# Reordering VectorE in a chunked WKV kernel: a state chain ahead of a rounding that waits for its load, and one rounding moved by a slot

## Chip, cores and metric

The kernel runs on one core of one Trainium2 chip. The metric is the device time of a run in microseconds. The time before is 293.12 us, the median of 3 runs (293.1 to 293.28). The profiled execution has a span of 292.3 us; times of day inside the trace are counted from the start of that span.

## The reference

For each of 16 sequences and each of 256 channels a recurrence runs over 2048 time steps. It keeps a numerator `aa`, a denominator `bb` and a running maximum `pp`:

```python
ww = u + kk;  qq = max(pp, ww)
e1 = exp(pp - qq);  e2 = exp(ww - qq)
output = (e1 * aa + e2 * vv) / (e1 * bb + e2 + 1e-08)
ww = pp - w + kk;  qq = max(ww, kk)
e1 = exp(ww - qq);  e2 = exp(kk - qq)
aa = e1 * aa + e2 * vv;  bb = e1 * bb + e2;  pp = qq
```

So every output is a weighted mean of the values v seen so far, with weights that decay by w a step and a bonus u for the present step. The inputs k and v and the output are 33.5 MB each.

## The kernel before

**Tiling.** The time axis is cut into 16 chunks of 128 steps, and a chunk into 4 pieces of 4 sequences each. A piece n (0 to 63) is a tile of 128 partitions (the steps) by 4 x 256 elements (sequence, channel), 512 KB for k and as much for v. Pieces n with the same n // 4 make up one chunk; four slots in a row are called a turn below.

**One piece.** Within a chunk the recurrence is done with matrices over the step axis. `round_k` (L176, VectorE) rounds k to the matmul's 32-bit type into `km`; `logs` (L185 and L191, TensorE) makes two tables of logarithms in PSUM banks 0 to 3; `exps` (L204, ScalarE) turns them into weights in the ring `EZR`, which holds 12 pieces; `cast_v` (L209, VectorE) rounds v to bf16 into `vb`; `times_v` (L214, VectorE) multiplies weights and v. `sums` (L238, TensorE) adds up the piece for the chunk's state.

**The outputs** follow LAG = 10 slots later. `den` (L341, TensorE) sums the denominators into banks 4 and 5; `recip` (L347 and L349, ScalarE) takes logarithm and exponential of the negative, that is the inverse, into `rd`; `num` (L354, TensorE) sums one half of the numerators into bank 6, and `mult` (L358, VectorE) multiplies that half by the inverse. Both halves use the one bank, so `num` of the second half waits for `mult` of the first, and so on. `store` (L361) writes `rd` out.

**The state.** Once per chunk a chain of small operations carries the state of the recurrence over: `copy_sums`, `turn`, `state_logs`, `state_frames`, `state_scan`, `state_offsets`, `state_weights` (L290, ScalarE, makes `G`), then `state_chain` (four VectorE operations, L299 to L304, the last of which writes `CB`), `turn_back` (L320, TensorE, transposes `CB`), `inject` (L326 on VectorE, then four small transfers, L331, into the ring's rows) and `state_next`. The next chunk's outputs need the injected rows.

**What sets the order.** The order of instructions is written out by hand: `K` keeps the program's order on each engine, and each engine takes its queue strictly in order. The table `plan` says, for each chunk, at which slot and at which named place of the slot each state function stands; `small_work(n, place)` runs what is due there. Slots 0 to 9 are a warm-up without outputs; slots 10 to 63 are the main loop; then come 11 short slots that only produce outputs. In the main loop VectorE's order in a slot is: `mult` of the first half (of piece n-11), the place "mid", `round_k(n+2)`, one, two or no `cast_v`, `mult` of the second half, the place "scan", `times_v(n)`, the place "chain". Before the change the casts stand as follows: slots with n%4 = 0 and 1 round v of piece n+1, n%4 = 2 rounds none, n%4 = 3 rounds v of n and of n+1.

**Loads and buffers.** The SP queue issues in slot n the load of v of piece n+5, the load of k of piece n+6 and the store of piece n-13, in that order. v has 5 load buffers, so the load of v(n+5) waits until `cast_v(n)` has read v(n); k has 6, and its buffer is freed by `round_k`, which runs two slots ahead of the piece. `vb` has 4 buffers and `rd` has 8.

For chunk 1 the chain is due at slot 10, the first of the main loop, at place "chain": behind `round_k(12)` and `times_v(10)`.

Of the kernel before, what the change touches and what calls it, by code (L numbers as in the profile page):

```python
# [15 lines left out]
def kernel(  # L16
# [17 lines left out]
    NP = 4 * NST  # L34
    RING = 12
    AHEAD = 6
    LAG = 10
# [29 lines left out]
    def load(n):  # L67
        if n - 1 < NP:
            load_v(n - 1)
        if n < NP:  # L70
            load_k(n)
# [3 lines left out]
    def matrix(name, dt):  # L75
        return consts.tile([128, 128], dt, tag=name, name=name)

    def fill(ap, value):
        K(DVE.memset(ap.bitcast(F32) if ap.dtype == F32R else ap, value))
# [68 lines left out]
    def out_matrices(*names):  # L148
        if "L" in names:
            for h in range(2):  # L150
                fill(Lx[HS * h:HS * h + HS, HS * (1 - h):HS * (2 - h)], 0.0)
        for name in names:
            x, f = I1 if name[0] == "I" else Lx, RS if name[-1] == "N" else 1.0
            mats[name] = matrix(name, BF16)
            K(DVE.tensor_single_scalar(mats[name], x, f, op=ALU.mult))
# [8 lines left out]
    DENB, NUMB, MISC = PS[:, 4:6, :], PS[:, 6, :], PS[:, 7, :]  # L164
# [6 lines left out]
    def ez(n):  # L171
        return EZR[:, :, n % RING]

    def round_k(n):
        km = consts.tile([128, 4, Dm], F32R, tag=f"km{n % 2}", name="km") if n < 2 else KM[n - 2]
        K(DVE.tensor_copy(km, kr_of.pop(n)))  # L176
        KM[n] = km

    def logs(n):
        km = KM[n].rearrange("p (i n) d -> p i (n d)", i=2)  # L180

        def rows(q):
            for i in range(2):
                g = 32 * (2 * q + i)
                K(PE.matmul(half(n, q)[:, i, :], CO[g:g + 32, :],  # L185
                            WU[g:g + 32, :].unsqueeze(1).broadcast_to([32, 2, Dm]), start=True, stop=False,
                            tile_position=(g, 0), skip_group_check=True))

        def steps(q):
            for i in range(2):  # L190
                K(PE.matmul(half(n, q)[:, i, :], (NLE, NLZ)[q], km[:, i, :], start=False, stop=True,  # L191
                            skip_group_check=True))

        rows(0)
        rows(1)
        steps(0)
        steps(1)

    def exps(n):
        if n < TURNS:  # L200
            for q in range(2):
                K(SC.activation(ez(n)[:, q], half(n, q), ACT.Exp))  # L202
        else:
            K(SC.activation(ez(n)[:, 0:2], PS[:, 0:4, :].rearrange("p (q i) x -> p q i x", q=2), ACT.Exp))  # L204

    def cast_v(n):
        vb = vbpool.tile([128, 4, Dm], BF16, tag="vb", name="vb")
        vr = vr_of.pop(n)
        K(DVE.tensor_copy(vb, vr))  # L209
        VB[n] = vb  # L210

    def times_v(n):
        vb = VB.pop(n).rearrange("p (i n) d -> p i (n d)", i=2)
        K(DVE.tensor_mul(ez(n)[:, 2:4], ez(n)[:, 0:2], vb.unsqueeze(1).broadcast_to([128, 2, 2, D])))  # L214
# [16 lines left out]
    def sums(n):  # L231
        c, p = divmod(n, 4)
        t = MISC[:, 0:Dm]
        for o in range(2):
            x = 24 - 16 * o - 2 * p
            for j in range(4):
                q, i = divmod(j, 2)
                K(PE.matmul(t[32 * j:32 * j + 32, :], mats["OH"][:, x:x + 32],  # L238
                            ez(n)[:, 2 * q, i, Dm * o:Dm * o + Dm],
                            start=p == 0 and o == 0, stop=p == 3 and o == 1,  # L240
                            tile_position=(0, 32 * j), skip_group_check=True))
# [102 lines left out]
    def recip(n, between=lambda: None):  # L344
        rd = rpool.tile([128, 2, D], F32, tag="rd", name="rd")
        for i in (slice(0, 1), slice(1, 2)) if n == NP - 1 else (slice(0, 2),):
            K(SC.activation(rd[:, i, :], DENB[:, i, :], ACT.Ln, scale=RS))  # L347
            between()
            K(SC.activation(rd[:, i, :], rd[:, i, :], ACT.Exp, scale=-1.0))  # L349
        RD[n] = rd  # L350

    def num(n, bank, i):
        for m, q in (("LN", 2), ("IdN", 3)):
            K(PE.matmul(bank, mats[m], ez(n)[:, q, i, :], start=q == 2, stop=q == 3, skip_group_check=True))  # L354

    def mult(n, bank, i):
        rd = RD[n]
        K(DVE.tensor_mul(rd[:, i, :], bank, rd[:, i, :]))  # L358

    def store(n):  # L360
        K(SP.dma_start(out=rows_of(out, n), in_=RD.pop(n).rearrange("p i (n d) -> p (i n) d", n=2)))  # L361
# [10 lines left out]
    for c in range(NST):  # L372
        s = 4 * c + 3
        plan = [(s + 1, "act" if s + 1 < LAG else "recip", copy_sums), (s + 1, "pe", turn),
                (s + 2, "act", state_logs), (s + 2, "mid", state_frames), (s + 2, "scan", state_scan), (s + 2, "scan", state_offsets),
                (s + 3, "recip", state_weights), (s + 3, "chain", state_chain),
                (s + 4, "nums", turn_back), (s + 4, "mid", inject), (s + 4, "mid", state_next)]
        if c == 0:
            plan = [(s + 1, "act", copy_sums), (s + 1, "pe", turn), (s + 1, "pe", state_logs),
                    (s + 1, "round", state_frames), (s + 1, "round", state_scan), (s + 1, "round", state_offsets),  # L380
                    (s + 2, "act", state_weights), (s + 2, "round", state_chain),
                    (s + 3, "pe", turn_back), (s + 3, "round", inject), (s + 3, "round", state_next)]
        if c == 1:
            plan = [(s + 1, "act", copy_sums), (s + 1, "pe", turn), (s + 2, "act", state_logs),
                    (s + 2, "round", state_frames), (s + 2, "round", state_scan), (s + 2, "round", state_offsets)] + plan[6:]
        if c == NST - 1:
            plan = [(s + 1, "copy", copy_sums), (s + 1, "turn", turn),
                    (s + 1, "post", state_logs), (s + 1, "mid", state_frames), (s + 1, "mid", state_scan), (s + 1, "mid", state_offsets),
                    (s + 2, "post", state_weights), (s + 2, "first", state_chain),
                    (s + 3, "turn", turn_back), (s + 3, "first", inject)]  # L390
        for slot, where, f in plan:
            later.setdefault((slot, where), []).append((f, c))

    def small_work(n, where):
        for f, c in later.pop((n, where), []):
            f(c)

    def idle_matmuls(n, bank):
        for _ in range(n):
            K(PE.matmul(bank, idle[:, 0:128], idle, start=True, stop=True, skip_group_check=True))  # L400
# [9 lines left out]
    for n in range(LAG):  # L410

        load(n + AHEAD)
        exps(n)
        if n % 4 == 0 and n:
            sums(n - 1)
        small_work(n, "act")
        small_work(n, "logs")
        logs(n + 1)
        if n % 4:
            sums(n - 1)  # L420
        small_work(n, "pe")
        idle_matmuls(2, NUMB)
        times_v(n)
        small_work(n, "chain")
        round_k(n + 2)
        small_work(n, "round")
        cast_v(n + 1)
        if n < 4:
            (state_start, lambda: out_matrices("L"), lambda: out_matrices("IdN", "LN"),
             lambda: out_matrices("Id"))[n]()  # L430
    for n in range(LAG, NP):

        q, qp = n - LAG, n - LAG - 1
        load(n + AHEAD)

        if qp >= 2:
            store(qp - 2)
        if qp >= 0:
            num(qp, NUMB, 0)
        den(q)  # L440
        small_work(n, "nums")
        exps(n)
        small_work(n, "act")
        if qp >= 0:
            mult(qp, NUMB, 0)
        small_work(n, "mid")
        if n + 2 < NP:
            round_k(n + 2)

        if n % 4 == 3:  # L450
            cast_v(n)
        if n + 1 < NP:
            if n % 4 != 2:
                cast_v(n + 1)
        else:
            times_v(n)
        if qp >= 0:
            num(qp, NUMB, 1)

        sums(n - 1)  # L460
        recip(q, lambda: small_work(n, "recip"))
        if qp >= 0:
            mult(qp, NUMB, 1)
        small_work(n, "scan")
        if n + 1 < NP:
            times_v(n)
            small_work(n, "chain")
            logs(n + 1)
        else:
            den(q + 1)  # L470
        small_work(n, "pe")
# [5 lines left out]
    for n in range(NP, NP + LAG + 1):  # L477

        q, qp = n - LAG, n - LAG - 1
# [52 lines left out]
```

## Time and profile before

| what | value |
|---|---|
| time, median of 3 | 293.12 us |
| span of the profiled execution | 292.3 us |
| busy: TensorE / VectorE / ScalarE / GpSimd | 257.5 / 261.9 / 258.4 / 113.9 us |
| moved by DMA, mean rate over the span | 101.53 MB, 347 GB/s |
| `cast_v` (L209) | 64 x 693 ns |
| `round_k` (L176) | 64 x 688 ns; its engine idle 2.3 us before it, for the load |
| `mult` (L358) | 118 instructions, mean 735 ns; its engine idle 13.8 us before it |
| `times_v` (L214) | 64 x 1227 ns |
| `exps` in the main loop (L204) | 54 x 1873 ns; idle 7.6 us before it |
| load of k or v, from issue to landing (median) | 8.3 and 8.2 us |

The profile is read like this. A timeline line gives the start in us, the duration, the engine, the line of the kernel, the operation, output and inputs, and in brackets how long the engine had been idle and what released it. "PE" is TensorE, "DVE" VectorE, "ACT" ScalarE, "POOL" GpSimd, "SPq" the queue that issues loads and stores. Durations on one engine overlap a little at their ends: a 128x1024 rounding has a record of 0.69 us, but the next instruction starts 0.60 us after it. In the windows view a line gives a stretch of the span, its length, the busy time and count of each engine (PE, PEld, DVE, ACT, POOL), then the granted TensorE clock, the share of the 16 DMA engines' time that packets took, and GB/s.

### The profile page before, as it was taken

Reading aid. Unit: us, or ns where it says so; the run is one execution under the profiler, and the core shown is the slowest. Engines: PE = TensorE matmul, PEld = TensorE weight load, DVE = VectorE, ACT = ScalarE, POOL = GpSimd, SP = SyncE. Lnnn points to the kernel's source line nnn. Section 1 sums busy time; section 2 is a strip of 40 time slices with the busy share of each in tenths; the row PEclk is TensorE's granted clock in tenths of the full one; section 3 lists DMA queues with packets and bytes.
Section 4 is the critical chain, followed back from the end, with each engine's and each line's share of the span. In section 5 each row is a group of like instructions: output and inputs, shape, how many; then the busy total and the mean of one; then the engine's idle time right before and its main releaser. Section 6 shows DMA issues by size and latency. Waiting matters only on the chain. (4 is left out here: it accounts for less than half of the span.)

```text
span 292.3 us, 4981 instructions
## 1 busy us (share of the span) xinstructions
PE 257.5 (88%) x1662; PEld 119.7 (41%) x1694; DVE 261.9 (90%) x453; ACT 258.4 (88%) x253; POOL 113.9 (39%) x212
## 2 busy tenths in 40 slices
PE   6976896998989899998989899998989899998881
PEld 2332442534444354444444354444444354433330
DVE  4698989899999999999999999999999999986853
ACT  2765685999999999999999999999999999999892
POOL 7000434153555535253555535253555535242200
PEclk9999997999999999999999999999999999999998
DMA  5999999999999999999999999999999999974686
GB/s 191 356 348 349 348 332 349 334 365 364 378 375 374 380 375 382 379 378 380 380 377 382 380 380 380 377 371 378 379 378 380 370 375 381 370 247 151 222 284 215
DMA packets 103521, 101.53 MB, mean 347 GB/s; under 512 B 4156, under 2 KB 103496, under 8 KB 103496
## 3 DMA queue, kind: packets, MB, share of 16 engines
q1 hardware_dynamic: 101144, 100.42, 100.7%
q0 software_dynamic: 2048, 0.53, 0.8%
q8 instruction: 13, 0.21, 0.3%
q10 hardware_dynamic: 304, 0.27, 0.3%
q14 instruction: 12, 0.10, 0.1%
HBM read 67.12 MB, written 33.55 MB: 344 GB/s over the span
## 5 line engine op out<-in xcount | busy, mean ns | idle before, releaser
L204 ACT ACTIVATE EZR<-PS 128x2048 bf16<-128x2048 f32 x54 | 101.1, 1873 | 7.6 <-PE PS L191 4.9
L358 DVE TENSOR_TENSOR rd<-PS,rd 128x512 f32<-128x512 f32 (+1 forms) x118 | 86.5, 735 | 13.8 <-PE PS L354 7.9
L214 DVE TENSOR_TENSOR EZR<-EZR,vb 128x2048 bf16<-128x2048 bf16 x64 | 78.5, 1227 | 0.7
L349 ACT ACTIVATE rd<-rd 128x1024 f32<-128x1024 f32 (+1 forms) x65 | 67.8, 1043 | 1.2
L347 ACT ACTIVATE rd<-PS 128x1024 f32<-128x1024 f32 (+1 forms) x65 | 65.6, 1010 | 1.4 <-PE PS L341 1.3
L331 POOL DMA_DIRECT2D EZR<-cb x64 | 40.1, 632 | 61.1 <-DVE cb L326 42.3
L354 PE MATMUL PS<-EZR,LN 128*128 128x512 bf16 x128 | 48.7, 380 | 12.8 <-DVE rd L358 10.0
L191 PE MATMUL PS<-km,NLE 128*128 128x512 f32 x128 | 47.2, 450 | 4.1 <-DVE km L176 4.1
L176 DVE CAST km<-kr 128x1024 fp32r<-128x1024 f32 x64 | 44.0, 688 | 2.3 <-DMA kr<-in_k_dram 2.3
L209 DVE CAST vb<-vr 128x1024 bf16<-128x1024 f32 x64 | 43.3, 693 | 2.7 <-DMA vr<-in_v_dram 2.4
L354 PE MATMUL PS<-EZR,IdN 128*128 128x512 bf16 x114 | 43.1, 378 | 0.0
L191 PE MATMUL PS<-km,NLZ 128*128 128x512 f32 x128 | 40.5, 398 | 0.0
L341 PE MATMUL PS<-EZR,L 128*128 128x512 bf16 x127 | 37.8, 378 | 1.8 <-ACT rd L347 1.8
L341 PE MATMUL PS<-EZR,Id 128*128 128x512 bf16 x114 | 35.0, 379 | 0.1
L269 POOL TENSOR_TENSOR F<-LL,LL 128x32 f32<-128x32 f32 x13 | 9.5, 733 | 62.0 <-ACT LL L260 62.0
L185 PE MATMUL PS<-WU,CO 32*128 32x512 bf16 x256 | 27.3, 388 | 3.1 <-DVE WU L406 1.6
L238 PE MATMUL PS<-EZR,OH 128*32 128x256 bf16 x512 | 26.3, 280 | 2.4 <-issue 0.4
L191 PEld LDWEIGHTS PS<-km,NLE 128*128 128x128 f32 x128 | 19.2, 190 | 19.2 <-issue 12.7
L191 PEld LDWEIGHTS PS<-km,NLZ 128*128 128x128 f32 x128 | 24.3, 190 | 5.7
L202 ACT ACTIVATE EZR<-PS 128x1024 bf16<-128x1024 f32 x20 | 19.4, 1019 | 7.9 <-PE PS L191 7.9
L354 PEld LDWEIGHTS <-IdN 128*128 128x128 bf16 x128 | 12.4, 97 | 26.1 <-issue 23.7
L354 PEld LDWEIGHTS <-LN 128*128 128x128 bf16 x128 | 12.8, 100 | 18.5 <-issue 11.5
(71 smaller groups left out, 204.5 us busy)
## 6 DMA issues: line engine op xcount, KB each, us to landing
kr<-in_k_dram SPq DMA_DIRECT2D x64, 512.0 KB, 8.3
vr<-in_v_dram SPq DMA_DIRECT2D x64, 512.0 KB, 8.2
out_dram<-rd SPq DMA_DIRECT2D x63, 512.0 KB, 8.1
EZR<-cb POOLq DMA_DIRECT2D x64, 8.0 KB, 5.2
out_dram<-rd SPq DMA_DIRECT2D x2, 128.0 KB, 3.1
out_dram<-rd ACTq DMA_DIRECT2D x2, 128.0 KB, 3.3
wuf<-in_w_dram ACTq DMA_DIRECT2D x1, 8.0 KB
wuf<-in_u_dram SPq DMA_DIRECT2D x1, 4.0 KB
```

The costliest lines, as they stand in the source:

```text
L176: K(DVE.tensor_copy(km, kr_of.pop(n)))
L185: K(PE.matmul(half(n, q)[:, i, :], CO[g:g + 32, :], WU[g:g + 32, :].unsqueeze(1).broadcast_to([32, 2, Dm]), start=True, stop=False, tile_p ...
L191: K(PE.matmul(half(n, q)[:, i, :], (NLE, NLZ)[q], km[:, i, :], start=False, stop=True, skip_group_check=True))
L204: K(SC.activation(ez(n)[:, 0:2], PS[:, 0:4, :].rearrange("p (q i) x -> p q i x", q=2), ACT.Exp))
L209: K(DVE.tensor_copy(vb, vr))
L214: K(DVE.tensor_mul(ez(n)[:, 2:4], ez(n)[:, 0:2], vb.unsqueeze(1).broadcast_to([128, 2, 2, D])))
L331: K(POOL.dma_start(out=EZR[r:r + 1, 2 * q, r0:r0 + 4, :, :].rearrange("o p i (b x) -> o (p i b) x", b=4), in_=cb[x:x + 32, :]))
L341: K(PE.matmul(DENB[:, i, :], mats[m], ez(n)[:, q, i, :], start=q == 0, stop=q == 1, skip_group_check=True))
L347: K(SC.activation(rd[:, i, :], DENB[:, i, :], ACT.Ln, scale=RS))
L349: K(SC.activation(rd[:, i, :], rd[:, i, :], ACT.Exp, scale=-1.0))
L354: K(PE.matmul(bank, mats[m], ez(n)[:, q, i, :], start=q == 2, stop=q == 3, skip_group_check=True))
L358: K(DVE.tensor_mul(rd[:, i, :], bank, rd[:, i, :]))
```

## The change

The change does two things, both to the order of work on VectorE.

First, chunk 1's state chain at slot 10 moves from behind `round_k(12)` and `times_v(10)` to the front of `round_k(12)`. That rounding waits for the load of k(12), and the chain needs only `G`. So that `G` is made before the chain in the program's order, the part of the slot that contains `recip` and `state_weights` is put into a function `inverses`, which slot 10 calls ahead of the rounding and all later slots at the old place.

Second, the rounding of v of a turn's first piece moves from the end of the turn before (n%4 = 3, where it made two casts behind `inject`) to its own slot (n%4 = 0). The casts are now: n%4 = 0 rounds v of n and of n+1, n%4 = 1 of n+1, n%4 = 2 none, n%4 = 3 of n. This spreads VectorE's work differently over the slots of a turn. It concerns 13 turns, from slots 11 and 12 to slots 59 and 60.

No instruction is added or removed, and the order on TensorE, ScalarE, GpSimd and the SP queue is unchanged.

```diff
         if c == 1:
             plan = [(s + 1, "act", copy_sums), (s + 1, "pe", turn), (s + 2, "act", state_logs),
-                    (s + 2, "round", state_frames), (s + 2, "round", state_scan), (s + 2, "round", state_offsets)] + plan[6:]
+                    (s + 2, "round", state_frames), (s + 2, "round", state_scan), (s + 2, "round", state_offsets),
+                    (s + 3, "recip", state_weights), (s + 3, "early", state_chain)] + plan[8:]
...
+    def inverses(n):
+        q, qp = n - LAG, n - LAG - 1
+        if qp >= 0:
+            num(qp, NUMB, 1)
+
+        sums(n - 1)
+        recip(q, lambda: small_work(n, "recip"))
+
     for n in range(LAG, NP):
...
         small_work(n, "mid")
+        if n == LAG:
+
+            inverses(n)
+            small_work(n, "early")
         if n + 2 < NP:
             round_k(n + 2)
 
-        if n % 4 == 3:
+        if n % 4 in (3, 0):
             cast_v(n)
-        if n + 1 < NP:
-            if n % 4 != 2:
-                cast_v(n + 1)
-        else:
+        if n + 1 == NP:
             times_v(n)
-        if qp >= 0:
-            num(qp, NUMB, 1)
-
-        sums(n - 1)
-        recip(q, lambda: small_work(n, "recip"))
+        elif n % 4 < 2:
+            cast_v(n + 1)
+        if n > LAG:
+            inverses(n)
```

## The prediction

> **What bounds the kernel now.** I read the page first, then the queue of each engine in order of time. The page says that three engines and the transfers are all nearly full, so shares alone decide nothing:
>
> ```profile
> PE 257.5 (88%) x1662; PEld 119.7 (41%) x1694; DVE 261.9 (90%) x453; ACT 258.4 (88%) x253; POOL 113.9 (39%) x212
> ...
> q1 hardware_dynamic: 101144, 100.42, 100.7%
> ```
>
> VectorE (DVE) in order of time shows the steady loop. A turn of four slots takes 16.43 us (the product at the head of slot 15 starts at 63.61, that of slot 19 at 80.05), and each turn has one gap, in the slot with n%4 = 1:
>
> ```profile
> 65.11 1.29 DVE L209 CAST vb<-vr 128x1024 bf16<-128x1024 f32 x2
> 66.32 0.68 DVE L358 TENSOR_TENSOR rd<-PS,rd 128x512 f32<-128x512 f32 x1
> ...
> 70.45 1.22 DVE L214 TENSOR_TENSOR EZR<-EZR,vb 128x2048 bf16<-128x2048 bf16 x1
> 72.12 0.69 DVE L358 TENSOR_TENSOR rd<-PS,rd 128x512 f32<-128x512 f32 x1 [0.46 <-PE PS L354]
> ```
>
> The product at 72.12 waits for TensorE, which is late because in slots 15 and 16 it waited itself for the products at 66.32 and 68.05; the first of them stands behind two roundings of v. So the loop runs DVE, PE, DVE, and the gap is what the bad order costs.
>
> The hand-over at slot 10 is the other place. DVE, ACT and PE there:
>
> ```profile
> 42.08 0.75 DVE L209 CAST vb<-vr 128x1024 bf16<-128x1024 f32 x1
> 43.63 0.70 DVE L176 CAST km<-kr 128x1024 fp32r<-128x1024 f32 x1 [0.81 <-DMA kr<-in_k_dram]
> 44.24 1.22 DVE L214 TENSOR_TENSOR EZR<-EZR,vb 128x2048 bf16<-128x2048 bf16 x1
> 45.38 0.22 DVE L299 TENSOR_TENSOR x<-AB,G 128x64 f32<-128x64 f32 x1
> ...
> 46.33 0.71 DVE L358 TENSOR_TENSOR rd<-PS,rd 128x512 f32<-128x512 f32 x1
> ```
> ```profile
> 42.40 0.37 ACT L290 ACTIVATE G<-A 128x192 f32<-128x192 f32 x1
> ...
> 50.99 1.88 ACT L204 ACTIVATE EZR<-PS 128x2048 bf16<-128x2048 f32 x1 [3.52 <-PE PS L191]
> ```
> ```profile
> 46.59 0.40 PE L320 MATMUL PS<-Id,CB 128*128 128x128 bf16 x4 [2.08 <-DVE CB L304]
> 47.10 0.41 PE L354 MATMUL PS<-EZR,LN 128*128 128x512 bf16 x1
> ```
>
> DVE idles 0.81 us for the load of k(12) although G is ready at 42.77; the chain then makes PE wait 2.08 us, and ACT 3.52 us.
>
> What decides the size is the loads. The windows of equal stretches (DMA share and GB/s are the last two columns) and the SP queue:
>
> ```profile
> 63.63:80.06 16.43, 15.29 (x104) 7.22 (x104) 15.82 (x28) 15.99 (x16) 7.60 (x13) 1.00 1.08 372
> ...
> 197.00:230.00 33.00, 30.76 (x209) 14.61 (x210) 31.82 (x54) 32.04 (x31) 15.32 (x27) 1.00 1.09 378
> ```
> ```profile
> 62.56 1.30 SPq L361 DMA_DIRECT2D out_dram<-rd  x1
> 65.83 0.37 SPq L64 DMA_DIRECT2D vr<-in_v_dram  x1
> 66.25 0.63 SPq L60 DMA_DIRECT2D kr<-in_k_dram  x1
> ...
> 242.58 1.24 SPq L60 DMA_DIRECT2D kr<-in_k_dram  x1
> ```
> ```profile
> 253.36 0.68 DVE L176 CAST km<-kr 128x1024 fp32r<-128x1024 f32 x1
> ```
>
> The transfers are saturated from 10 us on (share 1.08 to 1.09). The issue at 66.25 is k(21); that tile's view gives 7.4 us to landing, so it lands at 73.6 and is rounded at 80.95, 7.35 us later. The issue at 242.58 is k(63), the last; 8.1 us to landing, so 250.7, and it is rounded at 253.36: only 2.7 us spare. In 42 slots the spare time fell by 4.65 us, 0.44 us a turn. A turn of transfers (4 k, 4 v, 4 outputs) thus takes about 16.43 + 0.44 = 16.87 us, more than the compute's 16.43, which lives on loads fetched ahead.
>
> **What the Trainium skill says.** "TensorE: Matmul & The Clock Gate", Part 1: a free-running activity window of about 3.4 us decides whether the matmul clock is full or half. The trace agrees: the window 43.90 to 47.32 has 1.23 us of PE work, and the next, to 50.73, has a granted clock of 0.50. "Perfetto Trace Analysis", Identifying the Most-Contended Engine, warns that 16 DMA engines make occupancy misleading; so I judge by the falling spare time, not by the share. "DMA: Bandwidth & Descriptors", Issuing engines are not separate DMA queues: all transfers end on the same 16 engines, so reordering DVE work gives no more of them. Its Bandwidth section has 425 GB/s for 16 MB; no run here shows more than 382 in a slice, yet that leaves case C below open.
>
> **The change, part by part.** Nothing is added or removed: DVE has 430 instructions either way, and PE, ACT, POOL and SP keep their order.
>
> *Chain at slot 10.* The four chain operations cost 0.13 + 0.32 + 0.26 + 0.24 = 0.95 us from start to start (45.38 to 46.33). They now start at 42.83, when the rounding of v(10) ends, and end at 43.78. k(12) has landed by then (43.54), so 0.81 us of the chain lies in the idle time and the rounding of k is 0.15 us later. The first product moves from 46.33 to 43.78 + 0.61 + 1.14 = 45.53, 0.80 us sooner. PE no longer waits for CB; its numerator matmul follows that product, 46.26 in place of 47.10. From it to the next exponential took 3.89 us (47.10 to 50.99) with the half clock, against 2.62 (52.26 to 54.88) one slot later at full clock. If the half clock stays, slot 13 starts 0.8 us sooner. If the window gets enough work (1.23 + about 0.8 us), DVE runs on without waits: product 49.48, k 50.08, two roundings 50.68, product 51.88, 52.48, slot 13 at 53.62 in place of 55.59: 2.0 us. I take 1.4, the middle; ends 0.8 and 2.0.
>
> *Rounding of v moved.* One 0.60 us cast leaves slot 3 of each turn and joins slot 0. The product at 66.32 starts at 65.72, that at 68.05 at 67.45. PE's matmul after the latter goes from 68.79 to 68.18, its logs and turn follow, and the matmul at 71.42 can start at 70.8. The product at 69.85 keeps its place, now behind two casts, so its PE waiter (70.53 at the earliest) isn't delayed. The product at 72.12 starts at 71.59, when its own engine is free: the gap of 0.44 to 0.46 us is gone. The list of waits has 11 such gaps as "issue" (4.8 us) and two under PE; slot 13's is in the sum above, so 12 x 0.45 = 5.4 us. ACT has the room: its sequence of four slots has waits of about 0.2 us before three exponentials and one copy.
>
> *The wait it adds.* load_v(n+5) reuses the buffer of v(n). For n%4 = 0 that is now freed one slot later, so SP waits at slot 0 as it does at slot 3 (63.86 to 65.83), with the next load of k and a store behind it. In the old timing the issue at 67.94 would move to about 69.4. About six transfers of 1.4 us are outstanding (8.1 us to landing), so the engines don't run dry; and once compute is ahead, SP arrives later than the cast. I cost it at nothing, at worst 0.3 us a turn until about 160 us, where SP's idle time ends in the trace of before.
>
> *Sum.* Compute alone would gain 1.4 + 5.4 = 6.8 us (0.8 to 7.4). It can't have it. At slot 19 the spare is 7.35 us; it now falls by 0.45 + 0.44 a turn from 7.35 - 1.4, so it is used up 6.7 turns later, near slot 46 or 185 us. From there the rounding of k waits for its load in most slots. The end is then k(63)'s landing plus the unchanged rest, 292.3 - 253.36 = 38.9 us, which has no load of k. That rounding gains 2.7 us of spare plus what the transfers gain by SP no longer standing idle in the early turns: windows of 372, 375 and 378 against 379 GB/s, (7+4+1)/379 x 16.43 = 0.5 us. Against that, the later stretches, with the queue always full, run at 377 to 378 instead of 379 to 380: 0.5% of 65 us, 0.3 us. Gain 2.7 + 0.2 = 2.9 us: 293.12 - 2.9 = 290.2.
>
> **The rivals.**
> A, load floor as above: 290.2, or 289 to 291.4 for 1 us more or less in the landing of k(63). Chance 0.67. For it: the steadily falling spare.
> B, the gap moves instead of closing (another wait between DVE and PE, say behind the two casts in slot 0), only slot 10 gains: 293.12 - 0.8 to 2.0, so 291.7. Chance 0.12. Against it: each PE start above has room.
> C, transfers go faster when asked sooner, compute takes all: 293.12 - 6.8 = 286.3. Chance 0.11. For it: the 382 GB/s of the best slices, 1% above the mean; against it, SP without idle time after 165 us and still losing ground.
> D, the added wait of SP lets the transfers run thin, or the always full queue is slower: from k(21) at 73.6 on, at the 4.26 us a slot of the last 20 slots (k(43) to k(63)), k(63) lands at 252.5 and the time is still 292.3; with 0.3 us a turn of added idle over six turns it is 254.3, past 253.36 by 0.9: 294.1. Chance 0.10, of which 0.06 slower and 0.04 within 0.2%.
>
> **How the numbers follow.** A is the likeliest: 290.2. Faster 0.67 + 0.12 + 0.11 = 0.90, less 0.01 for the smallest end of B: 0.89. The range takes in A with its 1 us and the middle of B: up to 291.8. Downward, C's chance grows from A's edge; half of it left out gives 287.8.
>
> **What would show it.** Right: the chain stands before the rounding of k at 43.8 us; ACT's gap of 3.52 us shrinks by 0.8 to 2; the 0.44 us gap is gone in slots 1; waits of the rounding of k for its load go from 2.3 us in 3 to about 5 us in 12 or more, nearly all after 170 us; k(63) lands at 250 to 251 and is rounded at once; 39 us follow it. Wrong: no waits for k (B or C), the gap at another slot (B), k(63) landing 1 us or more off (C, D).

## The result and the profile after

The changed kernel takes 291.13 us (median of 4 runs, 290.98 to 291.18) against 293.11 us for the kernel before: ratio 0.9936, 95% interval 0.9918 to 0.9953, 2.0 us less. Forecast were 290.2 us and a range of 287.8 to 291.8. The direction, the range and the mechanism held; the gain was forecast 0.9 us too large. In a second measurement (after_again, below) it was 1.3 us, which lies at the upper edge of the range.

The page of the changed kernel, the same two lines as before:

```profile
PE 263.1 (91%) x1694; PEld 119.7 (41%) x1694; DVE 261.8 (90%) x453; ACT 256.2 (89%) x253; POOL 109.9 (38%) x212
...
q1 hardware_dynamic: 101144, 100.42, 102.0%
```

The work is the same: 32 of the 1694 matmul records are missing in the first trace, so TensorE's two busy figures can't be compared. The span is 3 us shorter; about 1 us of that belongs to the first profile, which was of a long execution (see b_again). VectorE (DVE) in order of time, slots 16 and 17, the place of the old gap:

```profile
65.58 1.29 DVE L209 CAST vb<-vr 128x1024 bf16<-128x1024 f32 x2
66.79 0.68 DVE L358 TENSOR_TENSOR rd<-PS,rd 128x512 f32<-128x512 f32 x1
67.39 1.22 DVE L214 TENSOR_TENSOR EZR<-EZR,vb 128x2048 bf16<-128x2048 bf16 x1
68.52 0.68 DVE L358 TENSOR_TENSOR rd<-PS,rd 128x512 f32<-128x512 f32 x1
```

The two casts now stand in the slot with n%4 = 0, and the product at 68.52 follows the multiplication after 1.13 us, without a wait. Before, 1.67 us lay between the same two starts (70.45 and 72.12). A turn is 15.89 us (60.55 to 76.44) instead of 16.43.

Slot 10, on DVE, on ScalarE (ACT) and on TensorE (PE):

```profile
41.42 0.74 DVE L209 CAST vb<-vr 128x1024 bf16<-128x1024 f32 x1
42.09 0.20 DVE L299 TENSOR_TENSOR x<-AB,G 128x64 f32<-128x64 f32 x1
...
42.79 0.45 DVE L304 TENSOR_TENSOR CB<-AB,G 128x128 bf16<-128x128 f32 x1
43.04 0.72 DVE L176 CAST km<-kr 128x1024 fp32r<-128x1024 f32 x1
...
44.80 0.68 DVE L358 TENSOR_TENSOR rd<-PS,rd 128x512 f32<-128x512 f32 x1
```
```profile
47.95 1.88 ACT L204 ACTIVATE EZR<-PS 128x2048 bf16<-128x2048 f32 x1 [1.21 <-PE PS L191]
```
```profile
45.54 0.38 PE L354 MATMUL PS<-EZR,LN 128*128 128x512 bf16 x1 [1.81 <-DVE rd L358]
```

The chain fills the wait for k(12); ACT's idle time fell from 3.52 to 1.21 us. PE no longer waits for `CB`, but still for the first product.

Then the loads. The list of DVE's waits, the view of k(63) alone, and DVE at its rounding:

```profile
DVE km L176 <- DMA kr<-in_k_dram: 6.0, 18, 0.5
```
```profile
L60 SPq DMA_DIRECT2D kr<-in_k_dram x1: 1274/1274/1274, 242.0 to 242.0; - x1
...
DMA to landing us min/median/max: 8.2/8.2/8.2
```
```profile
249.46 0.68 DVE L358 TENSOR_TENSOR rd<-PS,rd 128x512 f32<-128x512 f32 x1
250.23 0.73 DVE L176 CAST km<-kr 128x1024 fp32r<-128x1024 f32 x1
```

The rounding of k now waits 6.0 us for loads in 18 places (before: 2.3 in 3), three of them in the warm-up, the others after 148 us. k(63) is issued at 242.0, lands 8.2 us later, at 250.2, and is rounded at once; 0.77 us lie between the starts of the product and the rounding, where 0.60 is the distance without a wait. The stretches of a turn and of the later loop show the transfers full, as before:

```profile
60.55:76.44 15.89, 15.54 (x106) 7.16 (x104) 15.74 (x27) 15.78 (x16) 6.99 (x13) 1.00 1.09 374
193.00:226.00 33.00, 30.73 (x206) 13.89 (x206) 31.19 (x52) 30.53 (x30) 14.29 (x25) 1.00 1.09 376
```

### The profile page after: what moved, and what is told of

It is laid out like the page before. It is cut to its first block, busy times and chain, and to the rows that moved or that the text cites. A ratio compares the mean times of both kernels' runs of the same rounds, so it can differ in the third digit from the quotient of the medians.

```text
span 289.3 us, 5011 instructions
## 1 busy us (share of the span) xinstructions
PE 263.1 (91%) x1694; PEld 119.7 (41%) x1694; DVE 261.8 (90%) x453; ACT 256.2 (89%) x253; POOL 109.9 (38%) x212
## 5 line engine op out<-in xcount | busy, mean ns | idle before, releaser
L331 POOL DMA_DIRECT2D EZR<-cb x64 | 38.8, 612 | 56.3 <-DVE cb L326 43.2
L176 DVE CAST km<-kr 128x1024 fp32r<-128x1024 f32 x64 | 44.8, 699 | 6.4 <-DMA kr<-in_k_dram 6.0
L354 PE MATMUL PS<-EZR,IdN 128*128 128x512 bf16 x128 | 48.4, 378 | 0.0
L191 PE MATMUL PS<-km,NLZ 128*128 128x512 f32 x128 | 41.2, 404 | 0.0
L341 PE MATMUL PS<-EZR,Id 128*128 128x512 bf16 x128 | 38.1, 379 | 0.0
L269 POOL TENSOR_TENSOR F<-LL,LL 128x32 f32<-128x32 f32 x13 | 6.8, 525 | 62.0 <-ACT LL L260 62.0
L354 PEld LDWEIGHTS <-IdN 128*128 128x128 bf16 x128 | 12.5, 97 | 27.8 <-issue 25.2
L282 POOL TENSOR_TENSOR Q<-P,F 128x64 f32<-128x64 f32 x13 | 15.6, 1204 | 14.4 <-DVE P L273 14.4
```

What stands on the lines that cost most here:

```text
L331: K(POOL.dma_start(out=EZR[r:r + 1, 2 * q, r0:r0 + 4, :, :].rearrange("o p i (b x) -> o (p i b) x", b=4), in_=cb[x:x + 32, :]))
L341: K(PE.matmul(DENB[:, i, :], mats[m], ez(n)[:, q, i, :], start=q == 0, stop=q == 1, skip_group_check=True))
```

## The experiments

The theory: the loads set a floor. The last k lands when the saturated transfers have brought it, near 250 us, and 39 us follow; the change can take only the time by which the kernel before rounded it later. The rivals: the gain is limited on chip; or slot 10 or the turns bring their gain each by itself. The kernel before had medians of 293.09, 293.17 and 293.0 us in the three groups that follow (four experiments each, in this order). Single runs scattered by more than 1 us there, so each result has its ratio to the kernel before with a 95% interval; differences in us are between medians.

### The kernel before once more

No edit.

> The kernel before, unchanged, for a second profile: its profiled run in the first was 294.04 us, 0.9 us above the median of the timed ones, and its loads of the warm-up landed 1.0 us later than in the profile of the changed kernel. If that is chance of the start, this profile has a span of about 291.4 us and k(63) still lands 2.2 to 2.7 us before its rounding (load floor: the change can gain only this spare time). If the late start belongs to the kernel before, the span is 292.3 again and k(63) is rounded at 253.4.

The span is 291.2 us, as in the first case of the expectation. DVE at k(12) and at k(63), and the view of k(63), issued at 242.1:

```profile
42.60 0.69 DVE L176 CAST km<-kr 128x1024 fp32r<-128x1024 f32 x1 [0.41 <-DMA kr<-in_k_dram]
...
251.64 0.69 DVE L358 TENSOR_TENSOR rd<-PS,rd 128x512 f32<-128x512 f32 x1 [0.44 <-issue]
252.25 0.68 DVE L176 CAST km<-kr 128x1024 fp32r<-128x1024 f32 x1
```
```profile
DMA to landing us min/median/max: 8.1/8.1/8.1
```

k(63) lands at 250.2 as in the changed kernel and is rounded at 252.25, so 2.1 us are to spare, not 2.7. The first profile was of an execution of 294.04 us, 0.9 us above the timed median; in it the load of v(0) landed 1.1 us later (9.5 against 8.4), and k(12) 1.0 us later. Compute kept this delay to the end (k(12) was rounded at 43.63 against 42.60, k(63) at 253.36 against 252.25), but k(63) landed only 0.5 us later (250.65 against 250.18). So the first profile shows more spare time than the second, and it shows a wait of 0.81 us before the rounding of k(12) that is 0.41 us here.

### Each part alone, and both

Chain only, against the changed kernel:

```diff
-        if n % 4 in (3, 0):
+        if n % 4 == 3:
             cast_v(n)
         if n + 1 == NP:
             times_v(n)
-        elif n % 4 < 2:
+        elif n % 4 != 2:
             cast_v(n + 1)
```

> Only the first part: chunk 1's chain ahead of round_k(12); the casts as before. Load floor: the 2.1 us won at slot 10 fit into the spare time of the loads, so 293.1 - 1.5 to 2.1 = 291.0 to 291.6, with the 0.44 us gap of each turn still there and hardly a wait of round_k for its load. Rival, each part brings its share of the compute gain (1.4 of 6.8): 0.4 to 0.6 us, 292.6.

292.62 us, ratio 0.9987 (0.9974 to 1.0000): 0.47 us, and the interval reaches down to no gain. The load floor's 291.0 to 291.6 is missed; the number is the rival's. Yet it is not a share of a larger gain, and it isn't the loads that held it back: k(63) is rounded at 251.82, 1.9 us after it lands, and the 0.44 us gap stands in each turn. Slot 10 itself won only 0.4 us (k(15) is rounded at 54.68, in b_again at 55.08). ACT, and windows on either side of 46.8 us:

```profile
48.91 1.88 ACT L204 ACTIVATE EZR<-PS 128x2048 bf16<-128x2048 f32 x1 [2.09 <-PE PS L191]
```
```profile
43.41:46.82 3.41, 1.57 (x19) 0.58 (x19) 3.41 (x6) 3.38 (x3) 0.49 (x1) 0.99 1.09 348
46.82:50.24 3.42, 3.42 (x12) 1.77 (x9) 2.86 (x5) 1.33 (x2) 2.95 (x6) 0.51 1.09 349
```

The granted clock (third number from the end) is halved for 3.4 us, as in the kernel before.

Cast only, against the kernel before: the `cast_v` lines of the change, without the rest.

```diff
-        if n % 4 == 3:
+        if n % 4 in (3, 0):
             cast_v(n)
-        if n + 1 < NP:
-            if n % 4 != 2:
-                cast_v(n + 1)
-        else:
+        if n + 1 == NP:
             times_v(n)
+        elif n % 4 < 2:
+            cast_v(n + 1)
```

> Only the second part: the rounding of v moved by a slot; the chain as before. Load floor: compute gains 13 x 0.5 = 6.5 us but the loads allow 2.0 to 2.7, so 291.1 at best, the same as both parts together; waits of round_k for its load from about 190 us on; ACT's 3.5 us gap at 47 us stays. Rival, parts add up: both together minus the first part, 1.5 us at most, 291.6.

291.68 us, ratio 0.9950 (0.9930 to 0.9969): 1.41 us. The number alone is nearer to the rival's 291.6 than to 291.1. The trace shows the load floor: in the main loop the list of waits has 11 roundings of k that wait for their load, the first at 191.2 us (forecast: about 190), the last that of k(63), which had landed at 250.94:

```profile
250.12 0.68 DVE L358 TENSOR_TENSOR rd<-PS,rd 128x512 f32<-128x512 f32 x1
250.97 0.69 DVE L176 CAST km<-kr 128x1024 fp32r<-128x1024 f32 x1 [0.16 <-DMA kr<-in_k_dram]
```

Both parts, the changed kernel again:

> Both parts, the changed kernel once more beside the two parts alone. Load floor: 291.1, within 0.3 us of cast_only, k(63) rounded as it lands at about 250.2. Rival: below each part alone by about the other's gain, 0.5 us or more.

291.77 us, ratio 0.9965 (0.9945 to 0.9985), 1.32 us; k(63) lands at 251.10 and is rounded at 251.12. Both parts together are no faster than the second alone: 0.47 + 1.41 would have made 1.88, and the interval of both ends at 1.6 us. That sum is itself uncertain by more than half a microsecond, so the landings carry the argument: once the casts are moved, the loads are the floor, and slot 10 buys nothing that can be seen. This profile also has the half clock at slot 10, which the first profile of the changed kernel has not. First the windows of this run, then of the first profile:

```profile
42.71:46.12 3.41, 1.46 (x10) 0.59 (x9) 3.34 (x9) 3.41 (x3) 0.00 (x0) 1.00 1.09 349
46.12:49.54 3.42, 3.42 (x17) 1.49 (x17) 3.06 (x5) 1.16 (x2) 2.63 (x6) 0.50 1.09 350
```
```profile
42.71:46.12 3.41, 1.60 (x14) 0.66 (x16) 3.38 (x7) 3.38 (x4) 0.00 (x0) 1.00 1.09 347
46.12:49.54 3.42, 3.37 (x25) 1.53 (x24) 3.42 (x6) 2.21 (x2) 2.87 (x6) 1.00 1.09 348
```

The window is the same; the rounding of k(12) starts at 43.61 in the first of these two and at 43.04 in the second, where PE's work comes that much earlier. Whether that decides isn't shown (see the last section).

### The transfers relieved: half of the stores left out

In both kernels:

```diff
     def store(n):
+        if n % 2:
+            RD.pop(n)
+            return
```

> The kernel before without the stores of odd pieces in the loops (their outputs are left out): 10 instead of 12 transfers a turn, about 14.1 us against 16.43 us of compute. Load floor: compute set its pace already, so the turn stays at 16.43 us, the time within 0.5 us of 293.1, and k(63) has far more than 2 us to spare. Rival, compute itself is slowed by the transfers: clearly faster.

294.0 us, ratio 1.0026 (1.0009 to 1.0043). With two transfers of twelve gone, the turn stays at 16.42 us and k(63) has 9.7 us to spare: compute set its pace. That it is 0.8 us slower, outside the 0.5 us of the forecast, isn't explained; 0.6 us of it lies after the rounding of k(63), where 39.6 us follow instead of 39.0.

> The changed kernel without the same stores. Load floor: the loads no longer set the pace, and the whole compute gain shows: 0.5 to 2 us at slot 10 and 0.53 us in each of 12 turns, 6.9 to 8.4 us below half_stores_before, 285 to 286; no wait of round_k for its load after slot 12. Rival, the turns are bound by something on chip: 1.3 to 2 us below, 291.5.

286.61 us, ratio 0.9784 (0.9754 to 0.9814), 7.4 us below the one before it. A turn takes 15.89 us (76.71 to 92.60). DVE's waits:

```profile
DVE km L176 <- DMA kr<-in_k_dram: 1.0, 2, 0.7
```

Both waits are in the warm-up (the last before the rounding at 39.73, in slot 9); in the main loop none is left, k(63) has 8.9 us to spare, and the whole compute gain shows (7.4 us, forecast 6.9 to 8.4). This tells the load floor from a limit on chip: the same edit is worth 2.0 us with all stores and 7.4 us with half of them.

### Stores moved behind the last loads

Each store one slot later; buffers to hold the results longer:

```diff
-    vbpool = ctx.enter_context(tc.tile_pool(name="vbpool", bufs=4))
-    rpool = ctx.enter_context(tc.tile_pool(name="rpool", bufs=8))
+    vbpool = ctx.enter_context(tc.tile_pool(name="vbpool", bufs=3))
+    rpool = ctx.enter_context(tc.tile_pool(name="rpool", bufs=9))
...
-        if qp >= 2:
-            store(qp - 2)
+        if qp >= 3:
+            store(qp - 3)
...
-    store(NP - LAG - 3)
-    store(NP - LAG - 2)
+    for x in range(NP - LAG - 4, NP - LAG - 1):
+        store(x)
```

> The changed kernel with each store one slot later (9 rd buffers in place of 8, 3 vb in place of 4): one transfer of 1.4 us moves from ahead of the last loads to behind them. Load floor: k(63) lands 1.4 us sooner, so 1.2 to 1.5 us below the changed kernel, 290.2 in a batch with before at 293.1. Rival: same time as the changed kernel.

290.18 us, ratio 0.9897 (0.9878 to 0.9917): 3.0 us below before and faster than the changed kernel in either of its measurements. The one profile shows less than the medians: k(63) is rounded at 250.05, 0.2 us before the first profile of the changed kernel and 1.1 before the second. So the gain is measured, but that k(63) lands 1.4 us sooner isn't shown.

> The same edit on the kernel before. Load floor: its loads have about 2 us to spare, so nothing changes: 293.1 within 0.4 us, and the spare time of k(63) grows to about 3.4 us. Rival, later stores help by themselves: 1.4 us faster here too.

293.31 us, ratio 1.0007 (0.9995 to 1.0020). The same edit is worth nothing where the loads are not the floor. But the spare time didn't grow to 3.4 us: the landing of k(63) isn't on record here, and k(61) lands 2.4 us before its rounding, against 2.9 and 2.3 us in the two profiles of the kernel before. The start of the main loop shows where at least part of the 1.4 us went. The windows of b_again and of this run:

```profile
56.00:76.00 20.00, 19.21 (x128) 8.75 (x127) 19.39 (x32) 19.55 (x19) 10.40 (x18) 1.00 1.09 364
```
```profile
56.00:76.00 20.00, 18.79 (x126) 8.71 (x127) 19.40 (x33) 19.48 (x20) 10.09 (x17) 1.00 1.05 348
```

16 GB/s less over 20 us are 0.32 MB, by estimate 0.9 us of transfers at 377 GB/s (the first profile of the kernel before, which started as late as this run, also has 364). The likely reason is that the first stores come a slot later, while the next loads still wait for a free buffer. In the changed kernel the hole is smaller: 362 GB/s in defer1_after against 366 to 368 in the changed kernel and warm_after.

Two slots later (as above with `qp - 4` and nine `rd`):

> The changed kernel with each store two slots later (9 rd buffers, 3 vb): a second transfer of 1.4 us leaves the way of the last loads. Load floor: another 1.2 to 1.5 us below the one-slot version's 290.2, 288.9, unless the nine rd buffers now come free too late and ScalarE waits for a store, in which case it stays at 290.

290.64 us, ratio 0.9914 (0.9880 to 0.9947), not shown to be better than one slot. k(63) is rounded at 249.04, 1.0 us sooner than with one slot, but the list of ACT's waits has a new line:

```profile
ACT rd L347 <- DMA out_dram<-rd: 2.8, 7, 1.3
```

Nine buffers are too few: ACT waits for stores to leave, and 39.5 us follow the rounding of k(63), which starts 0.3 us after the landing.

Three slots later (`qp - 5`), with eleven `rd` paid for from the load buffers; shown against the version with two slots:

```diff
-    AHEAD = 6
+    AHEAD = 5
...
-    vpool = ctx.enter_context(tc.tile_pool(name="vpool", bufs=5))
+    vpool = ctx.enter_context(tc.tile_pool(name="vpool", bufs=4))
...
-    rpool = ctx.enter_context(tc.tile_pool(name="rpool", bufs=9))
+    rpool = ctx.enter_context(tc.tile_pool(name="rpool", bufs=11))
```

> The changed kernel with each store three slots later, 11 rd buffers, paid for by one k and one v buffer less (loads 5 and 4 pieces ahead instead of 6 and 5) and 3 vb. Load floor: three transfers moved, 4.2 us sooner for k(63), near the limit of compute that the kernel without half of its stores showed (286.6): 287.5. Rival, the loads need the sixth buffer: SP waits for the casts, the engines of the transfers run thin, and it is no faster than the two-slot version.

294.54 us, ratio 1.0048 (1.0032 to 1.0064): the rival. The waits of the SP queue, its issues around slots 10 to 12, and the windows there:

```profile
SPq L64 <- DVE vb L209: 26.6, 12, 7.3
```
```profile
42.73 1.42 SPq L60 DMA_DIRECT2D kr<-in_k_dram  x1
47.02 0.37 SPq L64 DMA_DIRECT2D vr<-in_v_dram  x1
47.44 0.52 SPq L60 DMA_DIRECT2D kr<-in_k_dram  x1
51.98 0.37 SPq L64 DMA_DIRECT2D vr<-in_v_dram  x1
```
```profile
46.00:52.00 6.00, 6.00 (x39) 2.37 (x37) 4.67 (x8) 3.32 (x3) 2.86 (x6) 0.72 1.10 341
52.00:58.00 6.00, 5.87 (x40) 3.27 (x37) 6.00 (x9) 5.97 (x8) 1.77 (x3) 1.00 1.01 312
```

SP stands idle for 2.9 us and 4.0 us before the two loads of v, waiting for a cast to free the buffer; the longest such wait, 7.3 us, follows before the load of v at 64.38. The rate falls to 312 GB/s (335 in warm_after of the next section, same stretch), and over 56 to 76 us it is 277, in warm_after 368; k(63) lands at 253.7. The shorter buffers aren't alone in this: with all load buffers kept, that stretch has 362 GB/s with stores one slot later and 346 with two. How the loss divides between buffers and later stores isn't shown. With the loads fully used, time in which they aren't asked for is lost for good.

### Slot 10 without the half clock

Five spare matmuls at the end of slot 10, in the changed kernel:

```diff
         small_work(n, "pe")
+        if n == LAG:
+            for _ in range(5):
+                K(PE.matmul(NUMB, mats["Id"], ez(n - 1)[:, 0, 0, :], start=True, stop=True, skip_group_check=True))
```

> The changed kernel with 5 spare matmuls (1.1 us) on TensorE at the end of slot 10, so that the activity window around 43 to 46 us has more work and the clock isn't halved in the next. Profiles so far show the half clock at about 46 to 50 us in some and not in others of the changed kernel. Expected: no half clock there, k(14) rounded at about 49.2 us. Load floor: the time stays that of the changed kernel (0.9935 to 0.9965 of before), for the loads end where they ended. Rival, slot 10 sets the time: 1 to 1.5 us faster than the changed kernel.

291.38 us, ratio 0.9945 (0.9926 to 0.9965): the changed kernel's time. The clock is full from 13.5 us to the tail, k(14) is rounded at 49.40, and k(63) lands at 250.69 and is rounded at 250.71. What slot 10 wins is waited for later.

> The version before this with the 5 spare matmuls at slot 10 too. If the loads no longer set the pace all the way, the 1.5 us of the half clock now count where that occurs: up to 1 us faster than without; if the loads still do, the same time.

293.99 us, ratio 1.0032 (1.0019 to 1.0046), against 1.0048 (1.0032 to 1.0064) without: the intervals overlap, so no effect of the spare matmuls is shown here either. k(63) is rounded at 253.30, and 39.0 us follow.

## Why the prediction was right, and where its size was off

**The bound** was read rightly. In five profiles with the moved casts (the changed kernel twice, cast_only, warm_after and defer1_after) the rounding of k(63) starts as it lands (defer1_after has no landing on record, but the rounding waits 0.2 us for the load), and 39.0 to 39.1 us follow, as after 252.25 and 253.36 in the kernel before (38.96 and 38.97). The sum "landing of k(63) plus an unchanged rest" is the whole time.

**The chain at slot 10.** Both ends of the forecast, 2.0 us at full clock and 0.8 at half, were a little high. From the rounding of k(12) to that of k(15) it is 12.5 us in b_again, 11.6 in chain_only (half clock) and 10.2 in the first profile of the changed kernel (full clock). The chain delays the rounding of k(12) itself by some 0.5 us from one profile to the next (42.60 to 43.12), where 0.15 was forecast: of the chain's 0.95 us, 0.81 were to fit into the wait for the load, but that was the late first profile, and b_again has only 0.41 us there. Net: 0.4 and 1.8 us. (The prediction's 430 VectorE instructions are 453 in both pages; nothing rests on it.)

**The cast.** The gap closed as forecast, and nothing took its place. It is worth 0.54 us a turn, not 0.45: 1.67 - 1.13 us from start to start. The 0.46 us in the brackets count from the end of a record, and records overlap the next start.

**When the spare time was used up** went with how much slot 10 gained. With the half clock (after_again) the first wait in the loop is that of k(48), close to the 185 us of the forecast:

```profile
186.57 0.79 DVE L176 CAST km<-kr 128x1024 fp32r<-128x1024 f32 x1 [0.25 <-DMA kr<-in_k_dram]
```

With the full clock it came earlier: the first k that is rounded as it lands is k(39) at 148.69 us in the first profile of the changed kernel and k(42) at 160.84 in warm_after.

**The added wait of SP cost nothing that shows.** SP's waits that end with a cast of v fell from

```profile
SPq L64 <- DVE vb L209: 17.6, 15, 1.9
```

in the kernel before to

```profile
SPq L64 <- DVE vb L209: 5.6, 7, 0.9
```

in the changed one, for compute runs ahead and SP arrives later than the cast. The shorter buffers of defer3_ahead5 show what such a wait costs when it does bind.

**The step that failed is the term "2.7 us of spare plus 0.2 us".** The mechanism was right, two sizes were not. The spare time was taken from a profile whose execution was 0.9 us above the median from which it was subtracted. In the second profile it is 2.07 us. Taken from its own execution, the first profile gives 294.04 - 2.71 = 291.3 us, close to the 291.13 measured. The transfers gained nothing by SP no longer standing idle: k(63) lands at 250.65 and 250.18 in the kernel before, 249.90 with the chain alone, 250.94 with the cast alone, 250.20, 251.10 and 250.69 in the changed kernel and its warmer version. That is a scatter of 1.2 us; with the casts moved the mean is 250.7, without it 250.2, so nothing came sooner, and that it came later isn't shown. So the gain is 2.1 us plus or minus that scatter; 2.0 was measured first, 1.3 in the second group.

**The rivals.** B (the gap moves) is refuted by the timeline, C (transfers go faster when asked sooner) by the landing times. D's slower full queue isn't shown either: 374 and 376 GB/s after, 372 and 378 before.

## What to carry to other kernels

When transfers are saturated, follow one late load through the whole program: the time between its landing and its use is all that faster compute can gain if the load lands no sooner, whatever the gaps on the engines add up to. Then look for transfers that can go behind the last load: stores one slot later gave another 1 to 2 us here, and only after compute had become faster than the loads. Look then at the place where the stores used to begin: if the loads there wait for buffers, the engines run thin and part of the gain is lost. Take the spare time and the time from the same execution, or from several; here one profile was off by 0.6 us on a gain of 2.

## What was not expected

The half clock at slot 10 comes and goes between executions of the same kernel, and the busy time of PE, as the profile models it, doesn't tell when. Around slot 10, windows with 1.23, 1.46 and 1.57 us of PE work out of 3.41 were followed by half the clock, and one with 1.60 us by the full clock. But the full clock also followed 1.57 us in defer1_after (window 42.48 to 45.90), and the half clock followed 1.89 us in defer1_before, in the warm-up:

```profile
26.66:30.07 3.41, 1.89 (x8) 0.86 (x8) 2.93 (x7) 1.91 (x4) 0.00 (x0) 1.00 1.09 349
30.07:33.48 3.41, 3.41 (x21) 1.17 (x20) 3.21 (x6) 1.91 (x2) 0.08 (x1) 0.50 1.09 347
```

So no threshold can be read from these runs. From the rounding of k(12) to that of k(15) the half clock cost 1.4 us (11.65 us in after_again, 10.24 in the first profile of the changed kernel), and keeping the clock full (warm_after) didn't change the time.

Leaving out half of the stores made the kernel before no faster; it was 0.26% slower, and the 39 us behind the last load of k became 39.6. The cause is open.
